# One decoder layer on one core: the border between output projection and MLP put into a written order on four engines

## The chip, the cores and the metric

The kernel runs on 1 core of one Trainium2 chip. The metric is the device time of one execution in microseconds (us), and less is better. Matrix products run on TensorE (PE), elementwise work on VectorE (DVE), ScalarE (ACT) and GpSimd (POOL), and nearly all DMAs are issued by SyncE (SP).

## The reference

One layer of a hybrid decoder on 1024 tokens of width 1024: two token mixers (sparse attention and retention), a gated merge, then an MLP with squared ReLU, all in float32.

```python
mix = (jax.nn.sigmoid(gate_a) * (nsa_out @ w_proj_a[layer])
       + jax.nn.sigmoid(gate_b) * (ret_out @ w_proj_b[layer]))
x = x + mix @ w_out[layer]
h = rmsnorm(x, norm_mlp[layer])
x = x + jnp.square(jax.nn.relu(h @ w_up[layer])) @ w_down[layer]
```

The change concerns the place where `mix @ w_out` ends and `h @ w_up` begins.

## The kernel before, in words

**Numbers in two halves.** A float32 operand of a product is split into a high part, rounded by ScalarE to the matmul's format, and a low part, the difference, taken by VectorE. Each product of two operands is three matmuls: high by high, high by low, low by high. In the names of the tiles, `bh` and `bl` are the halves of an activation, `wh` and `wl` those of a weight, `raw` a weight as loaded.

**Output projection** (lines 1154 to 1166). The result x1 has 8 tiles of 128 tokens and two halves of 512 columns. For each half the weights are split into four pairs of tiles (`out_w`), and a tile takes 24 matmuls (`dense_tok`). Behind each tile VectorE adds the residual x (L1163), SyncE stores the sum, and ScalarE takes the sum of its squares into `ssx` (L1166). A queue of delayed work, `later(d, fn)`, is served by `tick()` after every sixth matmul: the fourth tick of a tile ends it. After three ticks, that is, 18 matmuls into the next tile, `put_t` transposes the tile on TensorE (L1119, `tp`) and VectorE multiplies it by the norm's gain (L1123). The first half of the columns gives tiles `y1`, the second `y2`.

**The forms of the MLP's input.** The MLP's first product is a blocked product with fewer multiplications (Strassen's scheme): tokens are cut into tiles 0 to 3 and 4 to 7, columns into `y1` and `y2`, and seven products per pair of weight tiles replace eight. Beside the four plain blocks (11, 21, 12, 22) the scheme needs sums. When a first tile j < 4 is there, two of its blocks are split into `bh`/`bl` (forms 11 and 21). When a second tile j is there, all blocks of the tile pair (j-4, j) are: differences give form 2 (`t2h`, `t2l`), form 3 (`t3*`), form 4 (`t4*`), form 1 and form 22 (both in `bh`/`bl`). High parts are on ScalarE (L1113), low parts on VectorE (L1114), except that GpSimd takes the low part of form 1 (L1114) and one difference (L1140). In the second half of the columns the tiles run in the order 0, 1, 4, 2, 5, 3, 6, 7, and every piece of this work is put in the program behind the transposes of its tile.

**The first MLP products.** The MLP's hidden units come in 16 pairs of weight tiles. For the first two pairs, the two products that need forms 11 and 21 alone (`up_first`, `up_c11`) run as "heads" right behind the eighth tile: four products of 12 matmuls, which cover the work on the last tile. The other five products of a pair (`up_rest`, on forms 2, 3, 1, 4 and 22, in this order) need sums of weights: four instructions on the raw weights (`sf`, L1185 to L1188, three on GpSimd and one on VectorE), which are then split (`split_t1024`, L1029 and L1030). These sums are computed in `up_weights`, for the first pair behind the heads in the program.

**What sets the order.** Only TensorE's order is the order of the code (`manual_schedule` with PE, for the whole kernel). The order on VectorE, ScalarE, GpSimd and SyncE is chosen by a scheduler from its own costs. Each engine then runs its instructions strictly in that order, and an instruction that waits holds up all behind it. Buffers: three tiles for loaded weights (`raw`), five slots for split weights taken in turn, three tiles for x1 (`x1t`), four PSUM tiles for products (`mmu`) and four for transposes (`tp`), four tiles `y2`.

## Time and profile before

| | |
|---|---|
| time, median of 3 runs | 1602.65 us (1600.99 to 1603.06) |
| the profiled execution | 1602.7 us |
| its span, first to last instruction | 1600.9 us |
| busy: PE, DVE, ACT, POOL | 97%, 67%, 46%, 27% |
| granted TensorE clock, mean | 0.995 |

Times in the trace are counted from the span's start. The border of output projection and MLP lies at about 920 to 994 us: the tiles of the second half of the columns, the heads, and the first product on form 2. A row of the timeline gives start, duration, engine, line, operation, output and inputs, and in brackets how long the engine was idle just before it and what ended that. VectorE's and ScalarE's durations overlap a little from one instruction to the next, so what an instruction takes of the engine's time is the distance of two starts.

### The profile page before, as it was taken

The page shows a single profiled execution, that of the slowest core. Times are in us where ns is not written, and L with a number is a line of the kernel's source. Part 1 is how long each engine was busy: PE and PEld are TensorE (multiplying, and loading weights), DVE is VectorE, ACT ScalarE, POOL GpSimd, SP SyncE. Part 2 cuts the span into 40 slices and gives each one's busy share as a digit, 9 for nine tenths or more (in the row PEclk, how much of TensorE's full clock was granted, in tenths as well). Part 3 has the DMA queues.
Part 4 walks back from the last instruction along what each step waited for, and adds up shares of the span by engine and source line. Part 5 has one row for each costly group of instructions (what it writes and reads, how often), then busy time and mean ns, then how long its engine had stood idle before and what let it go on. Part 6 is the DMA issues. An engine that isn't in the chain of part 4 may idle for free.

```text
span 1600.9 us, 22753 instructions
## 1 busy us (share of the span) xinstructions
PE 1554.8 (97%) x7847; PEld 1298.4 (81%) x7847; DVE 1080.2 (67%) x2202; ACT 733.2 (46%) x1651; POOL 436.1 (27%) x516
## 2 busy tenths in 40 slices
PE   7999999999999999999999998999999999999997
PEld 5888887887888888888788876888888878888886
DVE  5765664674777877776656268777777658876673
ACT  5464454673767766676512134222222234443442
POOL 4110010001333323333000013655554426621320
PEclk9999999999999999999999999999999999999999
DMA  6102101252111111121544332444444498663472
GB/s 221 54 26 67 56 15 43 67 184 81 35 47 34 54 47 53 47 60 60 174 154 139 107 118 72 165 145 147 163 156 154 166 346 265 212 234 118 140 270 97
DMA packets 99427, 191.83 MB, mean 120 GB/s; under 512 B 26928, under 2 KB 30384, under 8 KB 99312
## 3 DMA queue, kind: packets, MB, share of 16 engines
q1 hardware_dynamic: 98752, 188.55, 35.8%
q0 software_dynamic: 560, 1.84, 0.3%
q8 instruction: 62, 1.02, 0.3%
q14 instruction: 53, 0.43, 0.1%
HBM read 140.02 MB, written 50.33 MB: 119 GB/s over the span
## 4 chain that ended last, share of the span: by engine, by line
PE 84%; DVE 5%; ACT 4%; issue 3%; POOL 2%; DMA 1%; POOLq 0%; ACTq 0%; DVEq 0%; SPq 0%
PE mmu L160 23%; PE mm L160 20%; PE mmd L160 18%; PE gps L160 8%; PE S L160 4%; PE O L160 3%; PE pt L894 2%; PE pt L893 2%; ACT pW L849 1%; DVE S L840 1%; PE pO L160 1%; DVE pl L896 1%; PE pc L160 1%; ACT pS L849 1%; DMA y<-w_down 0%
## 5 line engine op out<-in xcount | busy, mean ns | idle before, releaser
L1030 DVE TENSOR_TENSOR wl<-raw,wh 128x1024 fp32r<-128x1024 f32 x121 | 184.9, 1552 | 66.0 <-ACT wh L1029 65.8
L1029 ACT ACTIVATE wh<-raw 128x1024 fp32r<-128x1024 f32 x121 | 125.3, 1056 | 214.7 <-PE mmd L160 128.3
L160 PE MATMUL mm<-wh,bh 128*128 128x512 f32 (+1 forms) x448 | 175.4, 392 | 1.5 <-ACT n L581 1.0
L160 PE MATMUL mmd<-wl,wh 128*128 128x512 f32 x448 | 174.4, 389 | 1.6 <-DVE wl L1030 1.6
L160 PE MATMUL mm<-wh,bl 128*128 128x512 f32 (+1 forms) x448 | 170.1, 380 | 5.8 <-DVE bl L214 5.7
L160 PE MATMUL mmd<-wh 128*128 128x512 f32 x448 | 174.4, 389 | 0.9 <-DVE u L1216 0.9
L160 PE MATMUL mmd<-wh,wl 128*128 128x512 f32 x448 | 174.3, 389 | 0.0
L160 PE MATMUL mm<-wl,bh 128*128 128x512 f32 (+1 forms) x448 | 169.4, 378 | 0.0
L896 DVE TENSOR_TENSOR pl<-pt,ph 128x512 fp32r<-128x512 f32 (+1 forms) x160 | 103.7, 648 | 30.9 <-ACT ph L895 28.7
L895 ACT ACTIVATE ph<-pt 128x512 fp32r<-128x512 f32 (+1 forms) x160 | 90.5, 568 | 55.4 <-PE pt L894 52.5
L858 POOL TENSOR_SCALAR pS<-pS,cf 128x1024 f32<-128x1024 f32 (+7 forms) x64 | 48.1, 751 | 229.3 <-DVE cf L856 77.6
L840 DVE CUSTOM_DVE_ANT_0 S<-S,edge_m 128x512 f32<-128x512 f32 (+3 forms) x192 | 100.6, 530 | 14.2 <-PE S L160 12.4
L160 PE MATMUL gps<-bh,wh 128*128 128x512 f32 x256 | 108.3, 423 | 0.3 <-ACT gst L751 0.2
L160 PEld LDWEIGHTS mm<-wh,bl 128*128 128x128 f32 x448 | 84.7, 189 | 23.0 <-DVE bl L214 6.5
L160 PE MATMUL gps<-bl,wh 128*128 128x512 f32 x256 | 100.5, 393 | 0.0
L160 PE MATMUL gps<-bh,wl 128*128 128x512 f32 x256 | 100.5, 393 | 0.0
L160 PEld LDWEIGHTS mmd<-wl,wh 128*128 128x128 f32 x448 | 84.1, 188 | 19.6 <-DVE wl L1030 2.0
L160 PE MATMUL mmu<-bh,wh 128*128 128x512 f32 x256 | 99.7, 389 | 0.0
L160 PE MATMUL mmu<-bh,wl 128*128 128x512 f32 x256 | 99.6, 389 | 0.0
L160 PE MATMUL mmu<-bl,wh 128*128 128x512 f32 x256 | 99.6, 389 | 0.0
L160 PEld LDWEIGHTS mmd<-wh 128*128 128x128 f32 x448 | 84.1, 188 | 18.6 <-issue 1.3
L160 PEld LDWEIGHTS mmd<-wh,wl 128*128 128x128 f32 x448 | 84.1, 188 | 17.4
(318 smaller groups left out, 3962.2 us busy)
## 6 DMA issues: line engine op xcount, KB each, us to landing
raw<-u_scr SPq DMA_DIRECT2D x56, 512.0 KB, 3.8
raw<-w_down SPq DMA_DIRECT2D x41, 512.0 KB, 4.7
raw<-w_up SPq DMA_DIRECT2D x32, 512.0 KB, 3.6
u_scr<-u SPq DMA_DIRECT2D x60, 256.0 KB, 2.2
u_scr<-s SPq DMA_DIRECT2D x45, 256.0 KB, 2.0
y<-w_down SPq DMA_DIRECT2D x16, 512.0 KB, 6.9
x<-x SPq DMA_DIRECT2D x8, 512.0 KB, 3.7
qt<-q_scr SPq DMA_DIRECT2D x32, 128.0 KB, 2.4
```

The source lines that it names most:

```text
L160: T.matmul(o, w, m, start=start, stop=stop)
L840: V.tensor_tensor_reduce(sc, sc, mk, -0.125, BIGPOS, OP.add, OP.min, mx[:, b:b + 1])
L849: A.activation(o, sc, AF.Exp, bias=mx[:, m:m + 1], scale=-1.0, accum_out=sums[:, b:b + 1])
L858: G.tensor_scalar(v, v, cf[:, b:b + 1], 1.0, op0=OP.mult, op1=OP.mult)
L893: T.transpose(tp[:, bi * 2], p0, ident)
L894: T.transpose(tp[:, bi * 2 + 1], p1, ident)
L895: A.activation(ph[:, :n], tp[:, :n], AF.Copy)
L896: V.tensor_sub(pl[:, :n], tp[:, :n], ph[:, :n])
L1029: A.activation(h[:, :n], r, AF.Copy)
L1030: V.tensor_sub(l[:, :n], r, h[:, :n])
```

## The change

- In the second half of the columns, the heads and the first pair's `up_rest`, the order of PE, DVE, Activation and Pool is the order of the code (`border()`).
- The tiles of the second half run in the order 0, 4, 1, 5, 2, 6, 3, 7, so that each tile pair is complete one tile later; two tiles `y2` instead of four.
- The transposes of a tile come after two ticks (12 matmuls into the next tile), those of the last tile after one (6 matmuls into the first head).
- GpSimd does no low part, no difference and no weight sum in the border; VectorE does them. The low parts of a second tile are put behind the add of the next tile (`lows`).
- The first pair's raw weights are loaded during tile 0; their sums stand behind tile 5, and the split for the heads behind tile 6, the second pair's behind tile 7, followed by that of the sums.
- The second pair's weight sums and splits are woven into the first pair's five products (`mid`). From the third pair on the code does what it did, with GpSimd.

The core of the diff (the helper functions `load_up`, `up_sums`, `split_a` to `split_d` hold what `up_raw` and `up_weights` did, with the engine of the sums as an argument):

```diff
+BORDER = ('PE', 'DVE', 'Activation', 'Pool')
...
+        def up_sums(ra, rb, eng):
+            F = sfp.tile([P, 3, 512], F32, name="sf")
+            x11, x12, x21, x22 = ra[:, :512], ra[:, 512:], rb[:, :512], rb[:, 512:]
+            eng.tensor_tensor(F[:, 1], x11, x21, op=OP.subtract)
+            eng.tensor_tensor(x21, x21, x22, op=OP.add)
+            V.tensor_sub(F[:, 0], x21, x11)
+            eng.tensor_tensor(F[:, 2], x12, F[:, 0], op=OP.subtract)
+            return F
...
+        def border():
+            return tc.manual_schedule(engines={getattr(mybir.EngineType, e) for e in BORDER})
...
-            def split_ps(src, H, L, eng=None):
+            def high(key, src, H, L):
                 A.activation(H, src, AF.Copy)
-                (eng or V).tensor_tensor(L, src, H, op=OP.subtract)
+                low[key] = (L, src, H)
+
+            def lows(*keys):
+                for k in keys:
+                    L, src, H = low.pop(k)
+                    V.tensor_tensor(L, src, H, op=OP.subtract)
...
             def first_tile(j):
-                for c in range(2):
-                    ks = slice(4 * c, 4 * c + 4)
-                    split_ps(raw_t[j, c], bh[:, ks, cols(j)], bl[:, ks, cols(j)])
+                js = cols(j)
+                high("11", raw_t[j, 0], bh[:, :4, js], bl[:, :4, js])
+                high("21", raw_t[j, 1], bh[:, 4:, js], bl[:, 4:, js])
+                lows("11", "21")
+                V.tensor_sub(raw_t[j, 0], raw_t[j + 4, 0], raw_t[j, 0])
...
                 f2 = frm.tile([P, 4, P], F32, name="f2")
-                V.tensor_sub(y11, y12, y11)
                 V.tensor_sub(f2, y22, y11)
-                split_ps(f2, tf_[2][0][:, :, i], tf_[2][1][:, :, i])
-                G.tensor_tensor(y21, y21, f2, op=OP.subtract)
+                high("2", f2, tf_[2][0][:, :, i], tf_[2][1][:, :, i])
                 V.tensor_sub(y12, y22, y12)
-                split_ps(y12, tf_[3][0][:, :, i], tf_[3][1][:, :, i])
-                split_ps(y11, bh[:, :4, js], bl[:, :4, js], G)
-                split_ps(y21, tf_[4][0][:, :, i], tf_[4][1][:, :, i])
-                split_ps(y22, bh[:, 4:, js], bl[:, 4:, js])
+                high("3", y12, tf_[3][0][:, :, i], tf_[3][1][:, :, i])
+                high("1", y11, bh[:, :4, js], bl[:, :4, js])
+                if j == NT - 1:
+                    lows("2", "3")
+                V.tensor_sub(y21, y21, f2)
+                high("4", y21, tf_[4][0][:, :, i], tf_[4][1][:, :, i])
+                high("22", y22, bh[:, 4:, js], bl[:, 4:, js])
...
+            with border():
+                F = None
+                for n, j in enumerate((0, 4, 1, 5, 2, 6, 3, 7)):
+                    x1t, ps = x_tile(j, 1)
+                    dense_tok(ps, j, W)
+                    add_x(j, 1, x1t, ps)
+                    if n and n % 2 == 0:
+                        lows("2", "3", "1", "4", "22")
+                    if n < 7:
+                        later(2, lambda j=j, x=x1t: piece(j, x))
+                    if n == 0:
+                        ra0, rb0 = load_up(0), load_up(1)
+                    if n == 3:
+                        F = up_sums(ra0, rb0, V)
+                    if n == 5:
+                        split_a(ra0, Xs[0])
+                        ra1 = load_up(2)
+                split_a(ra1, Xs[1])
+                split_b(F, Xs[0])
+                later(1, lambda: put_t(x1t, 7, 1))
+                p1 = [headp.tile([P, 512], F32, name="p1") for _ in range(2)]
+                heads = [{"p1": t} for t in p1]
+                ps = prod(Xs[0][11], 11, True)
+                A.activation(p1[0], ps, AF.Copy)
+                second_tile(7)
+                up_c11(Xs[0], heads[0], True)
+                lows("1")
+                split_c(rb0, Xs[0])
+                ps = prod(Xs[1][11], 11, True)
+                A.activation(p1[1], ps, AF.Copy)
+                lows("4", "22")
+                up_c11(Xs[1], heads[1], True)
+                split_d(F, Xs[0])
...
+        with border():
+            rb1 = load_up(3)
+            F1 = []
+            up_rest(0, Xs[0], heads[0], True,
+                    (lambda: F1.append(up_sums(ra1, rb1, V)), lambda: split_b(F1[0], Xs[1]),
+                     lambda: split_c(rb1, Xs[1]), lambda: split_d(F1[0], Xs[1])))
```

More of the change, by code (lines that the diff above doesn't have):

```diff
@@ L30 @@
 LO = 3
+BORDER = ('PE', 'DVE', 'Activation', 'Pool')
 CS = 6
-FIN = ('PE', 'DVE', 'Activation')
 BTB = 3
@@ L1072, in half @@
             return s[0][:, e * 512:(e + 1) * 512], s[1][:, e * 512:(e + 1) * 512]
-        def up_raw(p):
-            ra = wraw.tile([P, 1024], F32, name="raw", tag="raw")
-            nc.sync.dma_start(ra, a["w_up"][:, 2 * p].rearrange("p a b -> p (a b)"))
-            sa = split_t1024(ra)
-            return ra, {11: half(sa, 0), 12: half(sa, 1)}
         def prod(X, yi, ticks=False):
@@ L1144, in second_tile @@
-                split_ps(y21, tf_[4][0][:, :, i], tf_[4][1][:, :, i])
-                split_ps(y22, bh[:, 4:, js], bl[:, 4:, js])
-            def out_tile(j, c, x1t):
-                put_t(x1t, j, c)
-                if c:
-                    (first_tile if j < 4 else second_tile)(j)
-            W = out_w(0)
-            for c in range(2):
-                cs = slice(c * 512, (c + 1) * 512)
-                order = (0, 1, 4, 2, 5, 3, 6, 7) if c else range(NT)
-                for n, j in enumerate(order):
-                    x1t = tmp.tile([P, 512], F32, name="x1t")
-                    nc.sync.dma_start(x1t, a["x"][j * P:(j + 1) * P, cs])
-                    ps = psW.tile([P, 512], F32, name="mmu", tag="mm")
-                    dense_tok(ps, j, W)
-                    if c == 0 and n == NT - 1:
-                        W = out_w(1)
-                    V.tensor_add(x1t, ps, x1t)
-                    nc.sync.dma_start(x1_scr[j, :, cs], x1t)
-                    later(T_LAG - 1, lambda j=j, c=c, x=x1t: out_tile(j, c, x))
-                    A.activation(ps, x1t, AF.Square, accum_out=ssx[:, c, j:j + 1])
@@ L1167, in hybrid_block @@
-            raws = [up_raw(0), up_raw(1)]
-            heads = [up_first(raws[p][1], True) for p in range(2)]
-            for p in range(2):
-                up_c11(raws[p][1], heads[p], True)
-            while due:
-                tick()
-            V.tensor_add(rr, ssx[:, 0], ssx[:, 1])
-            V.tensor_scalar(rr, rr, 1.0 / D, EPS, op0=OP.mult, op1=OP.add)
-            V.reciprocal(rr, rr)
-        sfp = e5.enter_context(tc.tile_pool(name="sfp", bufs=1, reuse_waits="tile"))
+                high("3", y12, tf_[3][0][:, :, i], tf_[3][1][:, :, i])
@@ new lines, in second_tile, with x_tile @@
+                high("1", y11, bh[:, :4, js], bl[:, :4, js])
[4 more added lines that the diff above has]
+                high("22", y22, bh[:, 4:, js], bl[:, 4:, js])
+            def x_tile(j, c):
+                x1t = tmp.tile([P, 512], F32, name="x1t")
+                nc.sync.dma_start(x1t, a["x"][j * P:(j + 1) * P, c * 512:(c + 1) * 512])
+                return x1t, psW.tile([P, 512], F32, name="mmu", tag="mm")
@@ new lines, in add_x @@
+            def add_x(j, c, x1t, ps):
+                V.tensor_add(x1t, ps, x1t)
+                nc.sync.dma_start(x1_scr[j, :, c * 512:(c + 1) * 512], x1t)
+                A.activation(ps, x1t, AF.Square, accum_out=ssx[:, c, j:j + 1])
+            W = out_w(0)
+            for j in range(NT):
+                x1t, ps = x_tile(j, 0)
+                dense_tok(ps, j, W)
+                if j == NT - 1:
+                    W = out_w(1)
+                add_x(j, 0, x1t, ps)
+                later(T_LAG - 1, lambda j=j, x=x1t: put_t(x, j, 0))
@@ new lines, in piece @@
+            def piece(j, x1t):
+                put_t(x1t, j, 1)
+                (first_tile if j < 4 else second_tile)(j)
+            with border():
+                F = None
+                for n, j in enumerate((0, 4, 1, 5, 2, 6, 3, 7)):
+                    x1t, ps = x_tile(j, 1)
+                    dense_tok(ps, j, W)
+                    add_x(j, 1, x1t, ps)
[26 more added lines that the diff above has]
+                split_d(F, Xs[0])
+                assert not due and not low
+                V.tensor_add(rr, ssx[:, 0], ssx[:, 1])
+                V.tensor_scalar(rr, rr, 1.0 / D, EPS, op0=OP.mult, op1=OP.add)
+                V.reciprocal(rr, rr)
@@ L1194, in ev, with up_rest, between @@
         def ev(name):
             return evp.tile([P, 512], F32, name=name)
-        def up_rest(p, X, s, first):
+        def up_rest(p, X, s, first, mid=()):
+            mid = iter(mid)
+            def between():
+                next(mid, lambda: None)()
             p1 = s["p1"]
@@ L1201, in up_rest @@
             V.tensor_add(q, ps, p1)
+            between()
             if not first:
@@ L1206, in up_rest @@
             V.tensor_add(u3, ps, q)
+            between()
             ps = prod(X[1], 1)
@@ L1211, in up_rest @@
             relu2(u22, u22)
+            between()
             ps = prod(X[22], 4)
@@ L1214, in up_rest @@
             relu2(u21, u21)
+            between()
             ps = prod(X[4], 22)
```

53 lines of the change are left out of this document (30 added, 23 removed).

## The prediction

> **What bounds the kernel now.** The page comes first, then the busy times by stretch.
>
> ```profile
> span 1600.9 us, 22753 instructions
> PE 1554.8 (97%) x7847; PEld 1298.4 (81%) x7847; DVE 1080.2 (67%) x2202; ACT 733.2 (46%) x1651; POOL 436.1 (27%) x516
> ...
> 920.00:994.00 74.00, 64.37 (x291) 51.75 (x290) 53.50 (x69) 28.73 (x53) 17.79 (x12) 0.98 0.28 94
> 994.00:1285.00 291.00, 291.00 (x1285) 240.75 (x1283) 213.99 (x247) 67.55 (x76) 149.69 (x108) 1.00 0.46 157
> ```
>
> In the last two rows the columns are the length, then the busy time of PE, PEld, DVE, ACT and POOL, then the clock. TensorE (PE) bounds the kernel; a change that leaves its matmuls alone can save only its idle time and its slow matmuls. The border of output projection and MLP lies in 920 to 994 us, and TensorE is busy for 64.37 of 74 us there. From 994 to 1285 us it never idles, so what the border saves moves all of that forward unchanged. The waits of TensorE from 860 to 1000 us are these:
>
> ```profile
> PE tp L1119 <- DVE x1t L1163: 4.8, 3, 2.0
> PE mmu L160 <- ACT wh L1029: 4.2, 1, 4.2
> PE mmu L160 <- DVE wl L1030: 0.6, 1, 0.6
> ```
>
> That is 9.6 us: three times the transposes of an output tile wait for its add on VectorE (DVE), then the first product of the MLP that needs weight sums waits for its weights. Two rows of the chain of waits give the undisturbed pace, and the timeline of TensorE gives the places:
>
> ```profile
> 930.39 0.44 PE tp L1119 x4
> 930.83 5.48 PE mmu L160 x24
> ...
> 937.98 0.40 PE L160 MATMUL mmu<-wh,bh 128*128 128x512 f32 x1
> ...
> 950.14 0.66 PE L1119 MATMUL tp<-ident,x1t 128*128 128x128 f32 x4 [1.99 <-DVE x1t L1163]
> ...
> 964.18 0.66 PE L1119 MATMUL tp<-ident,x1t 128*128 128x128 f32 x4 [1.97 <-DVE x1t L1163]
> ...
> 971.98 0.40 PE L160 MATMUL mmu<-bh,wh 128*128 128x512 f32 x1
> ...
> 977.12 0.66 PE L1119 MATMUL tp<-ident,x1t 128*128 128x128 f32 x4 [0.88 <-DVE x1t L1163]
> ...
> 988.79 0.50 PE L160 MATMUL mmu<-t2h,wh 128*128 128x512 f32 x1 [4.18 <-ACT wh L1029]
> ...
> 990.13 0.80 PE L160 MATMUL mmu<-t2h,wl 128*128 128x512 f32 x1 [0.61 <-DVE wl L1030]
> 990.73 0.63 PE L160 MATMUL mmu<-t2h,wh 128*128 128x512 f32 x1
> ...
> 993.86 0.39 PE L160 MATMUL mmu<-t3h,wh 128*128 128x512 f32 x1
> ```
>
> A tile takes 5.48 + 0.44 = 5.92 us and a matmul 5.48 / 24 = 0.228 us. The fourth tile of the second half begins at 937.98, so the eighth could end at 937.98 + 5 x 5.92 = 967.58. Four head products of 12 matmuls and one set of transposes (10.94 + 0.44 us) would bring the product on t2 to 978.96, and that on t3, 12 matmuls later, to 981.7. It began at 993.86. **The border loses 12.2 us**, in full: 9.6 us of waits, and 2.6 us of slow running behind them (0.63 us a matmul behind the 4.18 us wait, where it was 0.39 before; 0.66 us for transposes that had waited). This is the most that the change can win here.
>
> Why VectorE is late, from its timeline, with GpSimd (POOL) behind it:
>
> ```profile
> 938.17 0.69 DVE L1163 TENSOR_TENSOR x1t<-mmu,x1t 128x512 f32<-128x512 f32 x1 [0.70 <-PE mmu L160]
> ...
> 942.71 0.69 DVE L1123 TENSOR_TENSOR y<-tp,gcol 128x512 f32<-128x512 f32 x1
> 943.44 0.69 DVE L1138 TENSOR_TENSOR f<-y,y 128x512 f32<-128x512 f32 x1
> 944.05 0.68 DVE L1141 TENSOR_TENSOR y<-y,y 128x512 f32<-128x512 f32 x1
> 944.65 1.78 DVE L1114 TENSOR_TENSOR bl<-y,bh 128x512 fp32r<-128x512 f32 x1
> 946.36 0.68 DVE L1114 TENSOR_TENSOR t2l<-f,t2h 128x512 fp32r<-128x512 f32 x1
> 947.11 0.69 DVE L1114 TENSOR_TENSOR t3l<-y,t3h 128x512 fp32r<-128x512 f32 x1
> 947.72 1.77 DVE L1114 TENSOR_TENSOR t4l<-y,t4h 128x512 fp32r<-128x512 f32 x1
> 949.41 0.68 DVE L1163 TENSOR_TENSOR x1t<-mmu,x1t 128x512 f32<-128x512 f32 x1
> ...
> 944.28 1.61 POOL L1140 TENSOR_TENSOR y<-y,f 128x512 f32<-128x512 f32 x1 [7.53 <-DVE f L1138]
> ...
> 947.67 1.27 POOL L1114 TENSOR_TENSOR bl<-y,bh 128x512 fp32r<-128x512 f32 x1 [1.79 <-ACT bh L1113]
> ```
>
> The reader sees two things. The add of a tile (949.41) stands behind four low parts of a second tile; and two of these took 1.78 and 1.77 us, just those beside a GpSimd instruction, where their neighbours took 0.68. The groups of the border count such cases:
>
> ```profile
> L1114 DVE TENSOR_TENSOR bl<-y,bh 128x512 fp32r<-128x512 f32 x12 | 12.6, 1051 | 6.3 <-ACT bh L1113 6.3
> ...
> L1114 DVE TENSOR_TENSOR t4l<-y,t4h 128x512 fp32r<-128x512 f32 x4 | 4.9, 1228 | 0.0
> L1114 DVE TENSOR_TENSOR t3l<-y,t3h 128x512 fp32r<-128x512 f32 x4 | 3.9, 964 | 0.2
> L1114 DVE TENSOR_TENSOR t2l<-f,t2h 128x512 fp32r<-128x512 f32 x4 | 3.8, 952 | 0.0
> ```
>
> Over 0.68 each, these 24 low parts lost 4.5 + 2.2 + 1.1 + 1.1 = 8.9 us, or eight stretches of 1.1 us.
>
> **The change, part by part.** *GpSimd leaves the border.* Four low parts, four differences, and three weight sums for each of two pairs, 14 instructions, move to VectorE. VectorE starts one such instruction every 0.61 us (943.44 to 944.05), or 0.72 us if it needs the one before it (942.71 to 943.44). That adds 14 x 0.61 = 8.5 us, and the 8.9 us of stretch end. In total even; what counts is the order.
>
> *The add comes ahead of the low parts.* VectorE at the first second tile, before (tile 4; y2 and y1 are transposed tiles, the *l are low parts, x1t the add):
>
> ```order
> L1123 TENSOR_TENSOR y2_10691<-tp_10686,gcol_95 128x512
> L1138 TENSOR_TENSOR f2_10693<-y2_10691,y1_10289 128x512
> L1141 TENSOR_TENSOR y1_10437<-y2_10691,y1_10437 128x512
> L1114 TENSOR_TENSOR bl_93<-y2_10691,bh_92 128x4x128
> L1114 TENSOR_TENSOR t2l_10192<-f2_10693,t2h_10191 128x4x128
> L1114 TENSOR_TENSOR t3l_10194<-y1_10437,t3h_10193 128x4x128
> L1114 TENSOR_TENSOR t4l_10196<-y2_10609,t4h_10195 128x4x128
> L1163 TENSOR_TENSOR x1t_10665<-mmu_10667,x1t_10665 128x512
> ```
>
> and the same place in the change:
>
> ```order
> L1157 TENSOR_TENSOR y2_10654<-tp_10649,gcol_95 128x512
> L1172 TENSOR_TENSOR f2_10656<-y2_10654,y1_10292 128x512
> L1174 TENSOR_TENSOR y1_10440<-y2_10654,y1_10440 128x512
> L1179 TENSOR_TENSOR y2_10612<-y2_10612,f2_10656 128x512
> L1189 TENSOR_TENSOR x1t_10634<-mmu_10636,x1t_10634 128x512
> L1148 TENSOR_TENSOR t2l_10192<-f2_10656,t2h_10191 128x4x128
> L1148 TENSOR_TENSOR t3l_10194<-y1_10440,t3h_10193 128x4x128
> L1148 TENSOR_TENSOR bl_93<-y1_10292,bh_92 128x4x128
> L1148 TENSOR_TENSOR t4l_10196<-y2_10612,t4h_10195 128x4x128
> L1148 TENSOR_TENSOR bl_93<-y2_10654,bh_92 128x4x128
> ```
>
> All five low parts are now behind the add, and no wait on GpSimd is left in the row. ScalarE (ACT) has the high parts ready by then; its own rows are
>
> ```profile
> 943.44 0.63 ACT L1113 ACTIVATE bh<-y 128x512 fp32r<-128x512 f32 x1 [2.12 <-DVE y L1123]
> ...
> 953.02 0.60 ACT L1166 ACTIVATE mmu<-x1t 128x512 f32<-128x512 f32 x1 [0.82 <-DVE x1t L1163]
> 953.55 0.19 ACT L1166 ACTIVATION_READ_ACCUMULATOR mmu<-x1t 128x1 f32 x1
> ...
> 986.96 0.68 DVE L1187 TENSOR_TENSOR sf<-raw 128x512 f32<-128x512 f32 x1
> 987.68 1.06 ACT L1029 ACTIVATE wh<-sf 128x1024 fp32r<-128x1024 f32 x1 [5.84 <-DVE sf L1187]
> 988.77 1.31 DVE L1030 TENSOR_TENSOR wl<-sf,wh 128x1024 fp32r<-128x1024 f32 x1 [0.52 <-ACT wh L1029]
> ```
>
> *The timetable.* By the written order, an add starts 0.19 us after its tile ends (938.17 against 937.98) if VectorE is free. From the third tile's add (938.17) on I count VectorE instruction by instruction:
> - Behind a first tile's add are the five low parts, y2, two low parts, one difference: ten starts of 0.61 with the add, and 0.14 since the last low part waits for a 0.63 us high part. That is 6.24 us to the next add.
> - Behind tile 5's add are the four weight sums, y2 and three differences: six starts of 0.61 and three of 0.72, 5.82 us.
> - Behind tile 6's add is the split of the first weights: 0.69 (add) + 0.74 (square sum) + 1.06 (high part on ScalarE) + 0.04 of hand-over, then some 1.15 for the low part, 0.72, and three of 0.61: 6.2 us.
>
> So the adds start at 938.17, 944.41, 950.23, 956.47, 962.7 and 968.9. The tiles end, at 5.92 us each, at 937.98, 943.90, 949.82, 955.74, 961.66 and 967.58. VectorE is late by 0.3, 0.2, 0.5, 0.8 and 1.1 us. The transposes now come after 12 matmuls, 2.73 us, not after 18; an add that ends 0.73 us after its start hides while it is less than 1.8 us late, so no tile waits. The last tile's transposes stand only 6 matmuls behind it: wanted at 967.58 + 1.37 = 968.95, ready at 969.64. **A wait of 0.7 us is left**, 0.9 with slower transposes behind it.
>
> *The first pair's weight sums come 40 us sooner* (behind the add at 944.41, where the row of before is at 986.96). VectorE before (sf is the weight sums):
>
> ```order
> L1114 TENSOR_TENSOR t2l_10192<-f2_10945,t2h_10191 128x4x128
> L1114 TENSOR_TENSOR t3l_10194<-y1_10572,t3h_10193 128x4x128
> L1114 TENSOR_TENSOR t4l_10196<-y2_10836,t4h_10195 128x4x128
> L1104 TENSOR_TENSOR u11_10980<-mmu_10967,p1_10915 128x512
> L1175 RECIPROCAL rr_96<-rr_96 128x8
> L1094 SCALAR_TENSOR_TENSOR u11_10980<-u11_10980 128x512
> L1187 TENSOR_TENSOR sf_11012<-raw_11010,raw_10903 128x512
> ```
>
> The sums stood behind all forms of the last tile, and their split (987.68, 988.77) came last of all. In the change they are behind tile 5, and at the heads only the splits are left:
>
> ```order
> L1189 TENSOR_TENSOR x1t_10882<-mmu_10884,x1t_10882 128x512
> L1030 TENSOR_TENSOR wl_10925<-raw_10829,wh_10924 128x1024
> L1030 TENSOR_TENSOR wl_10929<-sf_10727,wh_10928 128x1024
> L1157 TENSOR_TENSOR y2_10946<-tp_10941,gcol_95 128x512
> L1172 TENSOR_TENSOR f2_10955<-y2_10946,y1_10403 128x512
> L1174 TENSOR_TENSOR y1_10577<-y2_10946,y1_10577 128x512
> L1148 TENSOR_TENSOR t2l_10192<-f2_10955,t2h_10191 128x4x128
> L1148 TENSOR_TENSOR t3l_10194<-y1_10577,t3h_10193 128x4x128
> ```
>
> From the add's end at 969.6: square sum and first high part to 971.4, two splits to 973.7, y2, f2, y1, t2l to 976.3, t3l to 976.9. The product on t2 begins at 967.58 + 10.94 + 0.44 + 0.9 = 979.9, so its operands are ready 3.6 us early. The wait of 4.2 us and the slow matmuls behind it go.
>
> *Costed at nothing.* The second pair's sums on VectorE: the five products of the first pair (60 matmuls, 13.7 us) cover them. From 976.9 VectorE needs seven starts and a split of 1.15 (982.3) for the last tile's rest, waits for product 2 until 983.0, and needs three starts, the sums (2.7), small ones (some 0.4), a start and a split: the second pair's first low part is there near 989.7, against 993.6 when its product is due. If this cover of 4 us goes, each us beyond it is a us of wait. The loads: the second half of the second pair's weights is issued by SyncE after tile 6 and waits there for a buffer until about 960; behind it stand only stores, as all loads of x are ahead. The order from the third pair on is as before.
>
> **Sum.** The product on t3 begins at 982.6 instead of 993.86: 11.3 us less. The profiled execution took 1602.7 us (span 1600.9 and 1.8 around it), against a median of 1602.65 shown. Forecast: 1602.7 - 11.3 = **1591.4 us**.
>
> [...] VectorE was busy for 53.5 of 74 us, and the change gives it 14 instructions more; the stretch rows say that as much comes back.
>
> [...]
>
> **The rivals.**
> 1. *VectorE is the bound more tightly.* In written order each instruction takes its full 0.69 us, not 0.61. From the third add to the last there are some 45 instructions: 3.6 us later. Waits then come to 4.3 us at the last two sets of transposes. Gain 12.2 - 4.3 - 0.4 = 7.5 us: 1595.2 us. For it: VectorE is without a gap over this stretch. Against: the rows at 943.44 to 944.65 start 0.61 apart. 0.12.
> 2. *The 8.5 us of moved work delay VectorE and nothing comes back where it counts.* 11.3 - 8.5 = 2.8 us: 1599.9 us, no measurable change. For it: where a product hid a stretched low part, its 1.1 us win nothing. Against: those at 944.65 and 947.72 stood ahead of a late add. 0.05.
> 3. *Slower: the stretch isn't GpSimd's.* If low parts take 1.77 us for another reason, all 28 of the change can (seven a pair). Without the last five, 23 x 1.09 = 25 us come ahead of the last add: 1616 us. It decides from about 13 stretched low parts on. Against: 946.36 and 947.11, low parts between two GpSimd instructions, took 0.68. 0.04.
>
> That GpSimd stays in the border is excluded by its order: its next instruction belongs to the third pair.
>
> **The numbers.** 0.2% (3.2 us) is about what a measurement of this kernel can tell from no change. The forecast has 0.79, and its own range is 1589.5 (no wait left, 1590.5, and 1 us for the spread of the runs) to 1593.5. With rival 1 and a little beyond, the range is 1589.5 to 1597. Faster is forecast and rival 1, 0.91; same is rival 2, 0.05; slower is rival 3, 0.04.
>
> **What would show it.** Right: no low part over 0.8 us in the border; no wait of transposes but the last set's, near 0.7 us; clock 1.00 throughout; the product on t3 11 us sooner; nothing new after it. Wrong: a wait of transposes at tiles 2 to 6 (VectorE bound), low parts of 1.7 us without GpSimd, or a wait at the second pair's products.

## The result, and the profile after

The changed kernel takes 1594.01 us (median of 4 runs, 1593.77 to 1594.85), the kernel before in the same comparison 1601.82 us (1600.47 to 1603.06, 4 runs). The ratio is 0.995 with a 95% interval of 0.9938 to 0.9962: 7.8 us faster. Forecast were 1591.4 us in a range of 1589.5 to 1597. The border did what was forecast to 0.2 us. Then 2.6 us were lost again, 300 us later, at a place the prediction had not looked at.

The page of the kernel after, its first rows, and the busy times by stretch (length; busy time of PE, PEld, DVE, ACT, POOL; clock; DMA share; GB/s):

```profile
span 1592.3 us, 22743 instructions
PE 1555.6 (98%) x7847; PEld 1299.9 (82%) x7847; DVE 1077.9 (68%) x2216; ACT 730.8 (46%) x1651; POOL 418.3 (26%) x502
...
920.00:994.00 74.00, 73.52 (x342) 60.54 (x341) 60.37 (x94) 30.97 (x57) 0.00 (x0) 1.00 0.33 111
994.00:1285.00 291.00, 287.67 (x1265) 237.31 (x1264) 211.57 (x242) 67.90 (x77) 156.99 (x113) 1.00 0.49 167
1280.00:1290.00 10.00, 7.50 (x25) 5.56 (x24) 7.95 (x7) 6.74 (x7) 3.65 (x6) 0.83 1.00 365
```

In the border TensorE is now busy for 73.52 of 74 us and GpSimd for none. The third row holds the surprise: of 10 us behind 1280, TensorE is busy for 7.50, at a clock of 0.83.

The waits of TensorE in the kernel after, from 860 to 1000 us and then from 1000 us to the end:

```profile
PE tp L1153 <- DVE x1t L1189: 0.5, 1, 0.5
...
PE mmd L160 <- ACT wh L1029: 1.7, 1, 1.7
PE mmu L160 <- DVE u L1284: 0.8, 1, 0.8
PE mmd L160 <- DVE wl L1030: 0.8, 1, 0.8
```

and behind 1000 us in the kernel before, where the border had 9.6 us ahead of them:

```profile
PE mmd L160 <- DVE wl L1030: 1.6, 1, 1.6
PE mmd L160 <- DVE u L1216: 0.9, 1, 0.9
```

To see where the time went I cut both traces at the same three instructions: the transposes near 924 us, the product on t3, and the first matmul of the down projection (`mmd`). TensorE's timeline after:

```profile
924.48 0.60 PE L1153 MATMUL tp<-ident,x1t 128*128 128x128 f32 x4
...
969.78 0.66 PE L1153 MATMUL tp<-ident,x1t 128*128 128x128 f32 x4 [0.48 <-DVE x1t L1189]
...
979.85 0.39 PE L160 MATMUL mmu<-t2h,wh 128*128 128x512 f32 x1
...
982.57 0.39 PE L160 MATMUL mmu<-t3h,wh 128*128 128x512 f32 x1
...
1274.72 0.39 PE L160 MATMUL mmd<-wh 128*128 128x512 f32 x1
```

and the two cuts of the kernel before that have not been shown:

```profile
924.30 0.60 PE L1119 MATMUL tp<-ident,x1t 128*128 128x128 f32 x4
...
1285.94 0.47 PE L160 MATMUL mmd<-wh 128*128 128x512 f32 x1 [0.88 <-DVE u L1216]
```

| us | start to transposes | border, to t3 | up products, to `mmd` | rest of the span |
|---|---|---|---|---|
| before | 924.30 | 69.56 | 292.08 | 314.96 |
| after | 924.48 | 58.09 | 292.15 | 317.58 |
| won | -0.18 | 11.47 | -0.07 | -2.62 |

The border wins 11.47 us, and the sum of the last row is the 8.6 us between the spans. The up products stand even because two things cancel: a new wait of 0.83 us at 1016 us, and the 0.88 us that the kernel before waited at 1285.94.

The loss in the rest of the span, in the chain of waits of the kernel after:

```profile
1271.97 8.88 DMA y<-w_down
...
1280.96 1.07 ACT wh L1029
...
1282.05 1.24 DVE wl L1030
```

and of the kernel before:

```profile
1282.15 7.55 DMA y<-w_down
...
1289.81 1.07 ACT wh L1029
...
1290.90 2.52 DVE wl L1030
```

The second weight group of the down projection is loaded into a buffer that comes free late among the up products; then it is split, and only then multiplied. After, this load begins 1274.72 - 1271.97 = 2.75 us ahead of the first `mmd`; before it was 1285.94 - 1282.15 = 3.79 us, mostly because the 0.88 us wait lay between. The load also takes 8.88 us, not 7.55, but that is not what the second wait grew by: from the load's start to the end of the low part it is 11.3 us in both traces. What stands there is GpSimd's last sum of the up products (first row before, second row after):

```profile
1291.02 1.30 POOL L1222 TENSOR_TENSOR s<-u,s 128x512 f32<-128x512 f32 x1
...
1280.84 1.27 POOL L1290 TENSOR_TENSOR s<-u,s 128x512 f32<-128x512 f32 x1
```

Before, the load landed sooner, and the low part, beside this sum, took 2.52 us; after, the low part began when the sum was nearly over and took 1.24 us. Its end lies 7.48 us behind the first `mmd` before and 8.57 us after. TensorE's timeline after shows the price:

```profile
1282.07 0.50 PE L160 MATMUL mmd<-wh 128*128 128x512 f32 x1 [1.74 <-ACT wh L1029]
1283.33 0.50 PE L160 MATMUL mmd<-wl,wh 128*128 128x512 f32 x1 [0.76 <-DVE wl L1030]
1283.66 0.46 PE L160 MATMUL mmd<-wh,wl 128*128 128x512 f32 x1
1283.92 0.63 PE L160 MATMUL mmd<-wh 128*128 128x512 f32 x1
1284.35 0.63 PE L160 MATMUL mmd<-wl,wh 128*128 128x512 f32 x1
...
1287.31 0.40 PE L160 MATMUL mmd<-wh,wl 128*128 128x512 f32 x1
```

The waits are 2.50 us, 0.9 more than the 1.6 before; behind them the matmuls start 0.43 us apart instead of 0.23 for eight of them, some 1.7 us. Together that is the 2.6 us.

### The profile page after: what moved, and what is told of

Read it like the earlier page. It is cut to its first block, busy times and chain, and to the rows that moved or that the text cites. A ratio compares the mean times of both kernels' runs of the same rounds, so it can differ in the third digit from the quotient of the medians.

```text
span 1592.3 us, 22743 instructions
## 1 busy us (share of the span) xinstructions
PE 1555.6 (98%) x7847; PEld 1299.9 (82%) x7847; DVE 1077.9 (68%) x2216; ACT 730.8 (46%) x1651; POOL 418.3 (26%) x502
## 4 chain that ended last, share of the span: by engine, by line
PE 84%; DVE 5%; issue 3%; ACT 3%; POOL 2%; DMA 2%; SPq 0%; POOLq 0%; ACTq 0%; DVEq 0%
PE mmu L160 22%; PE mm L160 20%; PE mmd L160 18%; PE gps L160 9%; PE S L160 4%; PE O L160 3%; PE pt L894 2%; PE pt L893 2%; ACT pW L849 1%; PE pO L160 1%; DVE S L840 1%; PE pc L160 1%; DVE pl L896 1%; DMA y<-w_down 1%; ACT pS L849 0%
## 5 line engine op out<-in xcount | busy, mean ns | idle before, releaser
L1111 POOL TENSOR_TENSOR sf<-raw 128x512 f32<-128x512 f32 x14 | 22.7, 1622 | 299.6 <-DVE wl L1030 294.7
```

The source lines that it names most:

```text
L1111: eng.tensor_tensor(F[:, 1], x11, x21, op=OP.subtract)
```

## The experiments

Twelve runs, the first of them the change once more, each timed in five rounds against the kernel before. In the text, "border" is the second stretch of the table above, read in each kernel's own trace at the same instructions, and "rest" the last one; before they are 69.56 and 314.96 us, after 58.09 and 317.58.

| | time, us | ratio to before, 95% interval | border | up products | rest |
|---|---|---|---|---|---|
| change again | 1593.16 | 0.9943 (0.993 to 0.9956) | 58.08 | 292.44 | 317.64 |
| TensorE alone in written order | 1590.8 | 0.9936 (0.9924 to 0.9949) | 58.42 | 291.04 | 317.64 |
| before, no GpSimd in the border | 1598.21 | 0.9975 (0.9966 to 0.9984) | 65.73 | 292.11 | 313.15 |
| change, sums late | 1600.21 | 0.999 (0.9981 to 0.9999) | 65.66 | 291.12 | 317.86 |
| before, sums early | 1598.52 | 0.9979 (0.9969 to 0.9989) | 68.45 | 292.07 | 313.08 |
| change, GpSimd back | 1593.28 | 0.9942 (0.9929 to 0.9956) | 59.35 | 291.04 | 317.60 |
| change, second group ahead | 1588.29 | 0.992 (0.9906 to 0.9933) | 58.10 | 292.23 | 312.87 |
| change, second pair woven | 1590.21 | 0.9927 (0.9915 to 0.994) | 58.07 | 291.04 | 315.98 |
| change, low parts first | 1597.06 | 0.9962 (0.995 to 0.9974) | 61.25 | 292.28 | 316.93 |
| the same with GpSimd | 1597.67 | 0.9973 (0.9963 to 0.9982) | 65.82 | 291.04 | 317.57 |
| three additions | 1587.31 | 0.9903 (0.989 to 0.9916) | 57.42 | 291.04 | 312.91 |
| three additions, TensorE alone | 1586.94 | 0.9905 (0.9891 to 0.9919) | 57.37 | 291.04 | 312.93 |

The start of the transposes near 924 us, ahead of everything that is changed, lies between 923.24 and 925.90 us in these traces. So a whole time moves by up to 2.7 us for reasons that have nothing to do with the edit, and the stretches are the finer measure.

**The change again.** Nothing is edited; the question is whether the loss behind the border comes back.

> The change itself, once more. In the first trace the product on t3 began 11.3 us sooner than before, and the last matmul only 8.6 us sooner: 1.0 us went at 1016 us (a wait for a PSUM buffer), 2.7 us at the next border near 1282 us, where a load of the second weight group of the next product landed late and the clock fell, and 0.9 us came back there. Theory A (the give-back belongs to the change: what waits at the next border is a transfer, which does not move forward with the matmuls): the same again, 8 to 9 us sooner than before, with the waits at both places. Rival B (chance of one execution): 10 to 11 us sooner, no fall of the clock at the next border.

Measured: 1593.16 us. The border is 58.08 us, the waits at the weight groups are there again (1.7 and 0.8 us), and the rest is 317.64 us. The loss of 2.6 us belongs to the kernel and not to one execution.

**TensorE alone in written order.** The code stays that of the change; VectorE, ScalarE and GpSimd go back to the scheduler, which had SyncE all along.

```diff
-BORDER = ('PE', 'DVE', 'Activation', 'Pool')
+BORDER = ('PE',)
```

> The change, but only TensorE's order is the order of the code; VectorE, ScalarE and GpSimd are left to the scheduler. In its order the splits of two weights stand ahead of the last tile's add. Theory A (the order is what wins): 2 to 4 us slower than the change, by waits of transposes for their add, the last set's above all. Rival C (leaving GpSimd is what wins, whatever the order): within 1 us of the change.

Measured: 1590.8 us, border 58.42 us, one wait of transposes of 0.8 us. The theory that the written order on VectorE carries the gain falls: it is worth 0.3 us in the border. The new code, with its tile pairs in turn, its low parts behind the add and its early sums, gives the scheduler an order that is as good: on VectorE it too has a tile's add (940.63) ahead of the low parts (from 941.24). The wait at 1016 us is missing here (291.04 us is what the up products take without any wait).

**The kernel before without GpSimd in the border.**

```diff
-                G.tensor_tensor(y21, y21, f2, op=OP.subtract)
+                V.tensor_tensor(y21, y21, f2, op=OP.subtract)
...
-                split_ps(y11, bh[:, :4, js], bl[:, :4, js], G)
+                split_ps(y11, bh[:, :4, js], bl[:, :4, js])
...
+            E = V if p < 2 else G
```

(`E` then takes the three sums of GpSimd.)

> The kernel before, with GpSimd's work in the border (low part of form 1, difference of form 4, weight sums of the first two pairs) on VectorE and nothing else changed. Theory A (order): the low parts lose their stretch of 1.1 us each, but the adds still stand behind them and the first pair's sums behind the last tile: 3 to 6 us faster than before, with waits of about 1 us left at two transposes and 2 to 3 us left at the product on t2. Rival C (leaving GpSimd alone wins): 8 us faster or more, like the change.

Measured: 1598.21 us, border 65.73 us, 3.8 us won. Its waits of TensorE from 860 to 1000 us:

```profile
PE mmu L160 <- ACT wh L1029: 3.9, 1, 3.9
PE tp L1119 <- DVE x1t L1163: 0.7, 3, 0.3
```

The waits of the transposes are gone, 4.8 us of them down to 0.7, with the low parts still ahead of the adds. The wait for the first weight sums is nearly as long as ever, 3.9 us, where 2 to 3 were expected. Theory A held in size, and rival C (leaving GpSimd is all of the gain) falls.

**The change with its sums late.** The first pair's sums and their splits stand behind the heads again, the rest is the change.

```diff
-                    if n == 3:
-                        F = up_sums(ra0, rb0, V)
...
                 up_c11(Xs[1], heads[1], True)
+                F = up_sums(ra0, rb0, V)
+                split_b(F, Xs[0])
+                split_c(rb0, Xs[0])
                 split_d(F, Xs[0])
```

> The change, with the first pair's weight sums and their splits behind the heads instead of behind tile 5. Theory A (the early sums remove the wait of 4.2 us and the slow matmuls behind it): VectorE comes to the sums near 983 us, their split is there near 987, against 979.9 when the product on t2 could begin; 6 to 9 us slower than the change at that product, as slow as before or nearly. Rival D (the sums are not what mattered, the waits of the transposes were): at most 2 us slower than the change.

Measured: 1600.21 us, border 65.66 us. Its waits from 860 to 1000 us:

```profile
PE mmu L160 <- ACT wh L1029: 4.7, 1, 4.7
PE tp L1153 <- DVE x1t L1189: 0.2, 1, 0.2
```

Theory A held, and rival D fell. Without the early sums 7.6 of the 11.5 us are gone: the 4.7 us wait, and slow matmuls behind it (clock 0.72 from 980 to 992 us).

**The kernel before with its sums early.** The other way round: only this part, on the kernel before.

```diff
+                    if c and n == 4:
+                        raw0 = up_raw(0)
+                        sums0(raw0[0])
-            raws = [up_raw(0), up_raw(1)]
+            raws = [raw0, up_raw(1)]
```

(`sums0` loads the second half of the weights and makes the four sums on VectorE in a buffer of its own; `y2` has three buffers, not four.)

> The kernel before, with one part of the change: the first pair's load and four weight sums come early, on VectorE, behind the fifth tile of the second half (a buffer of their own; y2 has three buffers instead of four). All else in the border is as before, GpSimd's low parts and differences, the lags and the scheduler's order included. Theory A (the sums' place is the main part: taking it out of the change cost 7.6 us at the first product on t3): the wait of 4.2 us for the high part of the sums at the first product on t2 goes or falls under 0.5 us, and with it the slow matmuls behind it; the waits of the transposes stay, 4 to 6 us in all, since the low parts still stand ahead of the adds; the first product on t3 comes 4.5 to 6 us sooner, the whole 1597 us (1596 to 1598.5), ratio near 0.997. Rival B (the parts only work together: with VectorE as late as before, four more instructions ahead of the last adds cost what the sums save): transposes wait 7 us or more, the product on t3 under 2.5 us sooner, 1600 us or more. Rival C (the sums alone are all of it): product on t3 over 9 us sooner, 1593 us.

Measured: 1598.52 us, but the border is 68.45 us, only 1.1 us shorter; the rest of the gain is in the stretch behind, where this trace has no wait at the weight groups. The wait for the sums is gone, and this is what took its place:

```profile
PE tp L1133 <- DVE x1t L1177: 7.2, 3, 3.2
```

Theory A fell, rival B held. Early sums alone put four instructions more ahead of adds that were late already. So the parts are not terms of a sum: in the border one part alone wins 1.1 us (sums early) or 3.8 us (GpSimd out), all but the early sums win 3.9 us, and together they win 11.5.

**The change with GpSimd back** for two instructions of each second tile.

```diff
-                    V.tensor_tensor(L, src, H, op=OP.subtract)
+                    (G if k == "1" else V).tensor_tensor(L, src, H, op=OP.subtract)
...
-                V.tensor_sub(y21, y21, f2)
+                G.tensor_tensor(y21, y21, f2, op=OP.subtract)
```

> The change, but of every second tile two of VectorE's instructions go back to GpSimd, as before: the low part of form 1 and the difference y21 - f2; order, sums and lags as in the change. The theory of the prediction (a VectorE instruction beside one of GpSimd takes 1.1 us longer, so that moving work to GpSimd saves VectorE 2 x 0.61 and costs it about 2 x 1.1 a tile pair): low parts of 1.7 us or more come back in the border, five to ten of them; VectorE is 1 us later a pair at most, and the slack of 1.8 us that the longer distance of the transposes gives hides most of it: waits of transposes 1 to 4 us in all instead of 0.5, whole 0 to 3 us longer than the change, 1593 to 1597 us. Rival B (GpSimd's absence is most of the gain, as in the before kernel, where the stretch came to 8.9 us): 6 to 9 us longer, 1600 us. Rival C (GpSimd takes work off VectorE and the stretch is as large as what it takes): no wait more, 1593 us, no difference.

Measured: 1593.28 us, no different from the change (1593.16). Groups of VectorE in its border:

```profile
L1148 DVE TENSOR_TENSOR t3l<-y,t3h 128x512 fp32r<-128x512 f32 x4 | 6.0, 1503 | 0.0
L1148 DVE TENSOR_TENSOR t2l<-f,t2h 128x512 fp32r<-128x512 f32 x4 | 5.8, 1439 | 0.1
L1148 DVE TENSOR_TENSOR t4l<-y,t4h 128x512 fp32r<-128x512 f32 x4 | 2.7, 680 | 0.0
```

The stretch is back: 4 x (0.82 + 0.76) = 6.3 us, against 8 x 0.61 = 4.9 us that GpSimd takes over. VectorE is 1.4 us worse off, and the border is 1.3 us longer; waits of TensorE there are 0.9 and 0.6 us. So the stretch is GpSimd's, as forecast, and in this order it costs 1.3 us in the border. The whole time is the same because this trace has no wait at 1016 us: its up products take 291.04 us, 1.1 us less than in the change. By the whole time the theory can't be told from rival C (no difference); the waits, 1.5 us instead of 0.5, speak for the theory.

**The change with the second weight group ahead.** This is aimed at the loss far behind the border.

```diff
+                t_raw1 = sfp.tile([P, 3, 512], F32, name="sf")[:, :2]
+                wsrc = a["w_down"].rearrange("p (q b) n -> p q b n", b=2)
+                nc.sync.dma_start(t_raw1, wsrc[:, 2:4, 0, :512])
...
+            if p == 15:
+                ahead[0, 1] = split_t1024(s_raw1)
+                ahead[1, 1] = split_t1024(flat(t_raw1))
```

> The change, with one thing more, far behind its border: the raw weights of the second group of the down projection's first two operands are loaded into a free buffer before the last up product, and both are split behind it, so that no load of that group waits for the last product's buffer. Theory A (what the change gives back at 1282 us is this load's latency of 8.88 us behind the product on form 4, then a split of 1.06 us): the waits of 1.74 and 0.76 us at the second group go, the clock stays at 1.00 from 1280 to 1290 us, and 2.5 to 4 us are won against the change: 1590 to 1591 us. Rival B (the transfers of that stretch are bound by what all 16 queues move there, 365 GB/s, so that the wait goes on to the third group): the waits move some us on, the whole within 1 us of the change. Rival C (the split of four more weight halves behind the last up products puts VectorE or ScalarE late): a wait of 1 us or more at the first down products, nothing won or slower.

Measured: 1588.29 us, 4.9 us less than the change run again (3.7 us by the ratios to the kernel before), and the rest is 312.87 us. From 1280 to 1290 us, where the change had 7.50 at 0.83:

```profile
1280.00:1290.00 10.00, 10.00 (x46) 8.29 (x45) 8.63 (x7) 6.98 (x7) 3.50 (x6) 1.00 0.99 363
```

and the only wait of TensorE left behind 1000 us is that at 1016:

```profile
PE mmu L160 <- DVE u L1284: 0.9, 1, 0.9
```

Theory A held and rival B (bound by the transfers) fell: the DMA engines move as much per second as before, 363 GB/s, and still nobody waits. It was the order of load, split and product; the edit moves load and split at once, so it does not tell the load from the split beside GpSimd. More was won (4.7 us in this stretch) than the 2.6 us that the change had lost there, since the kernel before had a wait of 1.6 us there itself.

**The change with the second pair woven.** The third pair's sums go to VectorE, between the second pair's products, in written order.

```diff
-        X, s = Xs[1], heads[1]
-        for p in range(1, 16):
...
+            up_rest(1, Xs[1], heads[1], True,
+                    (lambda: F2.append(up_sums(ra2, rb2, V)), lambda: split_b(F2[0], X),
+                     lambda: split_c(rb2, X), lambda: split_d(F2[0], X)))
+        s = up_first(X)
+        for p in range(2, 16):
```

> The change, with the second pair's products in written order as well: the third pair's weight sums go to VectorE, between the second pair's products as the second pair's between those of the first. Theory A (the wait of 0.83 us at 1016 us comes from the third pair's sums, which wait for GpSimd and stand ahead of the second pair's evictions on VectorE): the wait at 1016 goes, the first product of the down projection comes 1 us sooner; whole 1593 us, about 1 us less than the change, too small to be told from it by the whole time, so that the trace decides. Rival B (the cause is the load behind the sums, not the engine: GpSimd waited 4.84 us for it): the wait stays or moves to the third pair, 0.5 to 2 us.

Measured: 1590.21 us. The wait at 1016 us is gone; the up products take 291.04 us, 1.1 us less than in the change. The rest is 1.6 us shorter for another reason: the waits at the second weight group are there, but no slow matmuls behind them (see the last section). In the change VectorE's timeline at that place reads (`u` is the second pair's last eviction, `sf` a weight sum of the fourth pair; theory A had named the third pair's, whose part on VectorE ran at 999.04):

```profile
1014.85 0.69 DVE L1113 TENSOR_TENSOR sf<-raw 128x512 f32<-128x512 f32 x1 [5.09 <-POOL raw L1112]
1015.46 0.68 DVE L1284 TENSOR_TENSOR u<-mmu,q 128x512 f32<-128x512 f32 x1
```

VectorE stood for 5.09 us at a sum that needs GpSimd, with an eviction behind it that TensorE waits for, at the third pair's product on t3:

```profile
1016.19 0.50 PE L160 MATMUL mmu<-t3h,wh 128*128 128x512 f32 x1 [0.83 <-DVE u L1284]
```

Ahead of its own part of that sum GpSimd stood idle for 4.84 us, for a reason that this row does not name:

```profile
1012.16 1.28 POOL L1111 TENSOR_TENSOR sf<-raw 128x512 f32<-128x512 f32 x1 [4.84 <-issue]
```

Rival B put it down to the weights' load, and SyncE's rows fit that: it issues two loads of `w_up` at 1007.8 and 1008.2 us, behind the store of a sum that GpSimd ended at 1007.31, and they land 4.3 to 5.4 us later. In the weave GpSimd is through with the first pair's sums at 1002.3 us, so that engine and load both come sooner. That the wait is gone fits theory A in kind, with another pair's sum. But four other kernels lost this wait without the weave (their up products take 291.04 to 291.12 us), so neither the engine's share nor the load's is settled.

**The change with the low parts first.** One part is undone: the five low parts of a second tile stand ahead of the next add.

```diff
-                    if n and n % 2 == 0:
-                        lows("2", "3", "1", "4", "22")
...
                 high("22", y22, bh[:, 4:, js], bl[:, 4:, js])
+                if j < NT - 1:
+                    lows("2", "3", "1", "4", "22")
```

> The change, with one part undone: the five low parts of a second tile stand ahead of the next tile's add again, not behind it (three tiles; still on VectorE, still in written order, pairs in turn, sums early). Theory A (the place of the add is what lets TensorE run on): the adds of tiles 1, 2 and 3 come 5 x 0.61 = 3.05 us later; with the lateness of 0.2 to 0.8 us that they had and the 1.8 us that the transposes' distance hides, each costs a wait of 1.4 to 2 us, the transposes behind it run 0.2 us slower, and the work of VectorE between is not more, so that nothing adds up: three waits, 4 to 6 us in all, 1597 to 1599 us. Rival B (VectorE works nearly without a gap, its sum of work sets the pace and the order within a pair changes little, as the scheduler's order did): waits under 1.5 us in all, 1593 to 1595 us.

Measured: 1597.06 us, border 61.25 us, 3.2 us longer than in the change. TensorE's waits there:

```profile
941.46 0.66 PE L1153 MATMUL tp<-ident,x1t 128*128 128x128 f32 x4 [0.85 <-DVE x1t L1191]
954.59 0.66 PE L1153 MATMUL tp<-ident,x1t 128*128 128x128 f32 x4 [1.06 <-DVE x1t L1191]
967.95 0.66 PE L1153 MATMUL tp<-ident,x1t 128*128 128x128 f32 x4 [1.30 <-DVE x1t L1191]
```

Theory A held in kind: three waits at the three late adds. They are 0.85 to 1.30 us where 1.4 to 2 were expected. The distance of the transposes hides 1.8 us, as worked out; it is the adds that are less late. The first wait begins at 941.46 - 0.85 = 940.61, so its tile ended 2.73 us earlier, at 937.88, and the add could have started at 938.07. It started at 940.72, 2.65 us late; the other two, by the same working, 2.86 and 3.11 us, where 3.25 to 3.85 were expected. The whole lies at the lower edge of the expectation.

**The same with GpSimd back.** The edit of the sixth kernel on top of this one.

> The kernel with the low parts ahead of the adds, and of each second tile the low part of form 1 and the difference y21 - f2 on GpSimd, as before the change. With the low parts behind the adds these two made no difference in time. Theory A (the stretch counts where a late add waits for the stretched instructions): of the 8 instructions beside GpSimd's about 6 stand ahead of a late add now; 6 x 1.1 less the 6 x 0.61 that GpSimd takes over is 3 us more of waits than with all on VectorE, 1600 to 1602 us. Rival B (the two balance wherever they stand): within 1 us of the kernel with low parts first and no GpSimd.

Measured: 1597.67 us, 12 runs from 1595.77 to 1602.02; the intervals of this kernel and the last overlap. The profiled execution, with a span of 1599.5 us, is among the long ones. In its trace the three waits are longer by 1.0 us each:

```profile
943.48 0.66 PE L1153 MATMUL tp<-ident,x1t 128*128 128x128 f32 x4 [1.83 <-DVE x1t L1191]
957.59 0.66 PE L1153 MATMUL tp<-ident,x1t 128*128 128x128 f32 x4 [2.04 <-DVE x1t L1191]
971.95 0.66 PE L1153 MATMUL tp<-ident,x1t 128*128 128x128 f32 x4 [2.31 <-DVE x1t L1191]
```

That is the 3 us that theory A gave (stretch 8.1 us in its groups, less 4.9). Its whole time of 1600 to 1602 us was reached by some runs and not by the median. In this trace the clock falls as well, to 0.91 from 960 to 980 us, which makes up the rest of the 4.6 us in the border. Whether it falls in the other runs is not seen. So the mechanism is shown in the trace; in the whole time the two kernels differ by 0.6 us (medians) or 1.8 us (ratios), which is not clear of the noise.

**Three additions together**, once with all four engines in written order and once with TensorE alone: the second group ahead, the second pair woven, and the last transposes 12 matmuls behind their tile.

```diff
-                later(1, lambda: put_t(x1t, 7, 1))
+                later(2, lambda: put_t(x1t, 7, 1))
```

> The change with three things more: the second weight group of the down projection loaded and split ahead (it won 5 us), the second pair's products woven with the third pair's sums on VectorE (wait at 1016 us gone), and the last tile's transposes 12 matmuls behind it instead of 6 (wait of 0.5 us). If the three add up: no wait of TensorE from 860 to 1592 us but single ones under 0.5 us, clock 1.00, 1586 to 1588 us. Rival: the split of the last down groups or a load comes later instead, and the whole stays at that of the load ahead alone, 1588 to 1590 us.

> The same three things, with only TensorE in written order and the other engines in the scheduler's. If written order on VectorE and ScalarE is worth no more than 0.4 us, as the change alone said: within 1.5 us of the kernel with all engines in written order. Rival: the woven second pair needs the written order, and without it the scheduler puts the third pair's sums ahead of the evictions: a wait near 1016 us of 0.8 us or more, 1 to 2 us slower.

Measured: 1587.31 and 1586.94 us. From 860 us to the end neither has a wait of TensorE that the view of the waits lists. The border is 57.42 us, 12.1 us shorter than before, and the three add up. The two do not differ, so the rival for the second kernel falls: the scheduler's order has no wait at 1016 us either. These are the fastest kernels of the study, 15 us under the kernel before and 6 to 7 us under the change.

## Why the prediction was right, and where it was not

**The whole time: in the range, but not for the reason that the range gives.** 1594.01 us lies outside the forecast's own 1589.5 to 1593.5 us (the change run again, with 1593.16, just inside), in the part that was added for rival 1. Rival 1 did not happen. The border came out as forecast, and a loss that the prediction did not have brought the time there; that it stayed within the range is luck. Of the signs of being right, "nothing new after it" failed.

**The loss of the border, 12.2 us: right.** The kernel with three additions has no wait left there and its border is 12.1 us shorter.

**The timetable of VectorE: right.** I had the last two adds start at 962.7 and 968.9. VectorE's timeline after:

```profile
962.85 0.68 DVE L1189 TENSOR_TENSOR x1t<-mmu,x1t 128x512 f32<-128x512 f32 x1
963.45 0.68 DVE L1148 TENSOR_TENSOR t2l<-f,t2h 128x512 fp32r<-128x512 f32 x1
964.05 0.68 DVE L1148 TENSOR_TENSOR t3l<-y,t3h 128x512 fp32r<-128x512 f32 x1
...
969.05 0.68 DVE L1189 TENSOR_TENSOR x1t<-mmu,x1t 128x512 f32<-128x512 f32 x1
```

Starts are 0.60 us apart, no low part takes more than 0.69, and rival 1 (0.69 us each, more waits) is out. The wait of the last transposes is 0.48 us where 0.7 was forecast; with them six matmuls later it is gone. The product on t2 starts at 979.85 (forecast 979.9), that on t3 at 982.57 (982.6).

**The wait for the sums: right**, and undone alone it is the largest part: with the sums late again, 7.6 us return.

**"That adds 8.5 us, and the 8.9 us of stretch end": right, but it carried less than it seemed.** With GpSimd back for two instructions of a second tile, VectorE loses 1.4 us net and the border 1.3 us. Rival 2 (what comes back does not count) is out, with 11.5 us won; but in the change's order what comes back counts for little. It counts for more where low parts stand ahead of the adds: without GpSimd the border of the kernel before is 3.8 us shorter.

The stretch itself is in the rows: in the kernel before a low part of 128x512 takes 0.68 us alone and 1.77 us beside GpSimd, and with GpSimd back the low parts at 938.20 and 951.30 take 1.77 and 1.78 us beside its instructions, those behind them 0.68. Why VectorE is slower there, no run shows. Rival 3 is out: with GpSimd idle in the border no low part of the change takes more than 0.69 us.

**"What the border saves moves all of that forward unchanged": wrong, and this is the step that failed.** I read the row of 994 to 1285 us, saw TensorE without a gap, and took everything behind for a shift. The rest of the span is not: the second weight group is loaded, then split, then multiplied, and the first `mmd` does not wait for it. Before, 0.88 us of a wait just ahead of that `mmd` gave the group time. With the change this wait is gone; the three traces with the old code there have it, none with the new code has, and no run shows which part of the change took it. A wait of 0.83 us at 1016 us stands in its place in the sum, where it helps no load. So the group's low part was there 1.1 us later against the first `mmd`, the waits grew by 0.9 us, and the clock fell behind them (0.83 from 1280 to 1290 us). The forecast of 11.3 us lacked a term of -2.6 us. The kernel with this group loaded and split ahead shows it: the waits, the slow matmuls and 4.7 us of that stretch go together.

How large the term is depends on the trace that it is taken against. The kernel before without GpSimd in the border and the one with its sums early have the same code behind the border and the same 0.9 us of a wait ahead of the first `mmd`, but no wait at the group: their rest is 313.1 us, not 314.96. Against these two the change loses 4.5 us there.

**"The order from the third pair on is as before": wrong in effect.** A wait of 0.83 us came at 1016 us, in the third pair's products, behind the second pair's last eviction and a weight sum of the fourth pair. It went with the second pair woven, but it is missing too with TensorE alone in written order, with the sums late, with GpSimd back, and with the low parts first and GpSimd. So a small shift of the order is enough, and the one cause of this wait is not shown.

**Wrong in emphasis: the order by hand.** The prediction took the written order on four engines as what puts the add ahead of the low parts. With the scheduler on three of them the border was only 0.3 us longer. What counts is what stands where in the code, above all the low parts behind the add (3.2 us) and the early sums (7.6 us), not who fixes the order. The order of the tile pairs and the earlier transposes were not undone by themselves, so what each of these is worth is not shown.

## What to carry to other kernels

When an engine that is late causes two waits one behind the other, its parts cannot be priced one by one: removing one wait moves the lateness to the next, and only an edit that keeps both deadlines wins (the early sums alone 1.1 us, all but them 3.9, together 11.5). Follow a gain to the end of the trace: behind a busy stretch look for the next load that starts from a buffer's release and is waited for, since it can lose the slack that the old waits had given it. And read a gain in stretches between fixed instructions, where 0.3 us can be told, since the time ahead of the border alone differed by up to 2.7 us.

## What the runs showed of the hardware that was not expected

Short waits of the same sum brought slow matmuls in some traces and not in others. Behind 1.74 and 0.76 us (the change) matmuls start 0.43 us apart for 3.4 us. With the second pair woven the waits at the same place are 1.43 and 1.01 us, and what follows runs at full pace:

```profile
1279.75 0.49 PE L160 MATMUL mmd<-wh 128*128 128x512 f32 x1 [1.43 <-ACT wh L1029]
1281.26 0.50 PE L160 MATMUL mmd<-wl,wh 128*128 128x512 f32 x1 [1.01 <-DVE wl L1030]
1281.60 0.40 PE L160 MATMUL mmd<-wh,wl 128*128 128x512 f32 x1
```

So it is with the low parts first (0.47 and 1.98 us, clock 1.00). Six traces with waits of 2.4 to 2.5 us there have a clock of 0.83 in 10 us around them, these two have 1.00. What decides between the two outcomes, no run shows. For a forecast it means that waits of this size had two prices in these traces. From the first `mmd` to the last matmul it is 304.4 us in the three kernels with the group loaded ahead, 307.4 in the two with waits and a full clock, and 309.0 to 309.1 in the six: 3.0 us or 4.7 us.
